# Attention on one core: a written order table in place of a planner, 15 groups on VectorE instead of 16, the last pair dealt differently

## The chip, the cores and the metric

The kernel runs on one core of a Trainium2 chip. The metric is device time in microseconds, from launch to end, as a median of several runs. An execution recorded by the profiler gives the span of the core's instructions as well, and a trace of every instruction.

## The reference

```python
batch, heads, seq, dim = 8, 8, 512, 64            # q, k, v: float32
scale = 1.0 / np.sqrt(q.shape[-1])
scores = np.einsum('bhqd,bhkd->bhqk', q, k) * scale
attn = np.exp(scores - scores.max(axis=-1, keepdims=True))
attn = attn / attn.sum(axis=-1, keepdims=True)
return np.einsum('bhqk,bhkd->bhqd', attn, v).astype(np.float32)
```

There are 64 heads. For each, a 512x512 matrix of scores is formed, its exponential is taken, and the result, divided by its row sums, is multiplied with v.

## The kernel before

**Tiling.** The 64 heads are worked on as 32 pairs (0 to 31), the heads of a pair being a and b. The keys of a head are cut into four chunks of 128. A *block* is the transposed scores of one chunk of one head: 128 keys by 512 queries. Two blocks make a *group* of 128x1024, which is one score buffer (`st`, three of them, two PSUM banks each). In the plain pairs a group holds one chunk of both heads (a0b0, a1b1, a2b2, a3b3); in pair 0 and pair 31 it holds two chunks of one head (a0a1, a2a3, b0b1, b2b3). The two heads' q and k lie in different halves of the 64+64 partitions. There are 128 groups, m = 0 to 127; the last one, b2b3 of pair 31, is done in two halves of 256 queries each, which are steps 127 and 128. Groups 0 to 2 belong to a start written out by hand (`first_pair`).

**Stages, by engine.**
- SyncE loads q, k and v of a pair in 256 KB transfers (`load`, L509) into seven float32 buffers for each of the three, and stores the results from a ring of rows (`store`, L690 for two heads, L694 for one). The last two stores but one go through ScalarE's queue.
- GpSimd casts them to float16 (`cast`, L515 for v, L525 for q and k). `cast_behind` makes a cast wait for a chosen VectorE instruction, so that the two don't work on SBUF at the same time.
- TensorE transposes q and k of a pair (two steps of four, L558), VectorE copies them out of PSUM (`copy`, L565 for pair 1, L571), TensorE forms the scores of a group (two products, L598).
- ScalarE takes the exponential of a group out of PSUM (one instruction, L602, float16 out). For the groups in `ON_DVE` VectorE does this instead: a *raise* that makes float16 bits out of the scores (`raise_`, L625) and five *passes* that mend it (`pass_`, L642, L651, L659, L661, L665). Such a group is left as two factors, `pe` and `pd`, and each of its blocks is multiplied with v twice.
- TensorE multiplies the blocks with v and a column of ones (`values`, L704): a *unit* is one head's 128 queries, four products, and one more for each block that VectorE did. Seven units share a PSUM bank; VectorE takes the reciprocal of their sums (L671) and multiplies (L676). The last head has a path of its own (`last_values`, L720; `finish`, L733 and L734).

**What sets the order.** Every engine works off its own instructions in the order in which the program issues them. Before, the class `Plan` makes that order when the kernel is built: it steps through time with a cost for each operation, and at each step lets each engine choose by its own rules. Its list of steps is worked off in one loop, `for what, *args in steps: do[what](*args)`. A buffer of a pool goes to the next tile when the last reader issued for it has finished. Twelve exponentials (`KNOWN`) are made to wait also for the sixth-last cast issued before them (`OVER`).

The lines that say which groups go to VectorE, and which blocks a group holds:

```python
ON_DVE = (5, 10, 16, 25, 28, 39, 44, 54, 63, 66, 74, 81, 91, 96, 103, 116)
...
        if g in (0, LAST):
            stream += [(g, c, h) for h in range(2) for c in range(NI)]
        else:
            stream += [(g, c, h) for c in range(NI) for h in range(2)]
```

Of the kernel before, what the change touches and what calls it, by code (L numbers as in the profile page):

```python
# [17 lines left out]
class Plan:  # L18

    SLOT, EXP, EXP_DONE, EXP_FIXED = 216, 853, 181, 64  # L20
    INTO, OUT_OF = 96, 96
    TRANSPOSE, V_UNIT = 222, 128
    TO_ACT, TO_DVE, TO_PE = 220, 210, 60

    COPY, NORM, RAISE = (601, 690), (50, 133), (1132, 1215)
    RECIPROCAL = 115
    SCALE, PRODUCT, EXTRA = 333, 600, 29
    COPY_1 = (400, 190)
    NORM_COLUMN, PASS_DONE = 67, 115
    PASSES = (SCALE, SCALE, PRODUCT, SCALE, PRODUCT)  # L30
    BITS = 2
    NEEDS = (None, None, 0, 2, 3)
    FIRST_EXP = 5000
    STEP = 5
    CALM, KEEN = 9000, 4
    FIRST_UNIT = 4
    KNOWN, OVER = (13, 15, 18, 20, 22, 24, 27, 42, 50, 61, 69, 97), 6
    ON_DVE = (5, 10, 16, 25, 28, 39, 44, 54, 63, 66, 74, 81, 91, 96, 103, 116)

    LATE_NORM, LATE_COPY, HURRY, SOON, BACKLOG = 700, 1500, 800, 160, 600  # L40
    LATE_MUL, WAIT = 400, 200
    SLACK, AHEAD = 0, 2

    CAST, CAST_PORT, CAST_DONE, TO_POOL = 557, 475, 130, 150
    SCALE_PORT, PRODUCT_PORT, GAP, REACH = 271, 537, 20, 5
    FIRST_LAND, LOAD, STORE, LATENCY, ISSUE = 5200, 752, 376, 2300, 470
    QUEUED, URGENT = 3500, 16
    PAIRED, STORE_ISSUE = 18, 520
    RAW, QK16, NV, NU = 7, 5, 12, 112
    PAIR, DUEK, DUEV, DUEL, PRE = 3300, 3550, 6000, 5000, 0  # L50

    def __init__(self, groups, pairs, first):
        self.groups, self.pairs = groups, pairs
        self.pe, self.act, self.dve = 7000, self.FIRST_EXP, 6300
        self.pool, self.port, self.dma = 4600, 4600, self.FIRST_LAND
        self.m, self.tiled = first, True
        self.read = []
        self.exps = {}
        for m in range(first):
            self.act += self.EXP + self.EXP_FIXED  # L60
            self.exps[m] = self.act + self.EXP_DONE
            self.read.append(self.exps[m])
        self.tq = {0: 5800}
        self.transposed = {0: 5800}
        self.next_t = 1
        self.part_t = 0
        self.banks = [5100, 5800]
        self.todo = [(g, h) for g in range(pairs) for h in range(2)]
        self.last = self.todo.pop()
        self.last_part = 0  # L70
        self.head = None
        self.units = self.FIRST_UNIT
        self.member = {b: m for m, grp in enumerate(groups) for b in grp}
        self.ready = []
        self.passes = []
        self.passed = {}
        self.raised = set()
        self.steps = []
        self.busy_dve = 0
        self.order, self.paired = [], 0  # L80

        late = {grp[0][0] for m, grp in enumerate(groups) if m in self.ON_DVE}
        due = []
        for g in range(pairs):
            scores = 5000 + self.PAIR * g
            if g:
                due += [(scores - self.DUEK, g, "k"), (scores - self.DUEK + 10, g, "q")]
            due.append((scores + self.DUEV + (self.DUEL if g in late else 0), g, "v"))
        self.due = sorted(due)
        self.uncast = list(self.due)  # L90
        self.casts = []
        self.landed, self.cast_done = {}, {}
        self.first_loads = [(g, n) for _, g, n in self.due if g < self.RAW]
        self.first_loads += [(self.RAW, "k"), (self.RAW, "q")]
        for x in self.first_loads:
            self.dma += self.LOAD
            self.landed[x] = self.dma
        self.loads, self.stores, self.stored = [], [], []
        self.sp = 1650 + 470 * len(self.first_loads)

    def note(self, t, *what):
        self.steps.append((t, len(self.steps)) + what)

    def trigger(self, t):

        ops = self.ops
        if not ops or ops[-1][1] <= t - 300:  # L110
            return 1, None
        n = len(ops) - 1
        while (
            n > 0
            and len(ops) - n < self.REACH
            and not ops[n][2]
            and ops[n][0] - ops[n - 1][1] <= self.GAP
        ):
            n -= 1
        if n > 0 and ops[n][0] - ops[n - 1][1] <= self.GAP:  # L120
            n -= 1
        return len(ops) - n, ops[n][1]

    def emit(self, t, back, after):
        _, g, n = self.uncast.pop(0)
        shared = (g, n) == (1, "q")
        self.note(t, "cast", g, n, back if t > self.CALM else 0)
        if not shared:
            self.casts.append((g, n, t if after is None else after + self.TO_POOL))
        if g + self.RAW < self.pairs:  # L130
            self.loads.append((g + self.RAW, n))

    def fits(self, t, soon=0):
        if not self.uncast:
            return False
        _, g, n = self.uncast[0]
        if n != "v" and g >= self.QK16 and self.transposed.get(g - self.QK16, 1e9) > t:
            return False
        return self.landed.get((g, n), 1e9) <= t + soon

    def step_pool(self, t):
        if self.uncast and self.uncast[0][1:] != (1, "q") and not self.casts and self.pool <= t:
            quiet = not self.passes and self.port <= t and not any(x[1] == "raise" for x in self.ready)
            if self.fits(t) and (quiet or self.uncast[0][0] - self.PRE < t):
                self.emit(t, 1, None)
        if self.casts and self.pool <= t and self.port <= t:
            g, n, after = self.casts[0]
            if after <= t and self.landed.get((g, n), 1e9) <= t:
                self.casts.pop(0)
                begin = max(self.pool, self.port, after, self.landed[(g, n)])  # L150
                self.pool = begin + self.CAST
                self.port = begin + self.CAST_PORT
                self.cast_done[(g, n)] = begin + self.CAST + self.CAST_DONE

    def step_sp(self, t):
        if self.sp > t or (self.loads and self.dma > t + self.QUEUED):
            return
        urgent = len(self.stores) > self.URGENT
        if self.loads and not urgent:
            g, n = self.loads[0]  # L160
            if self.cast_done.get((g - self.RAW, n), 1e9) <= t:
                self.loads.pop(0)
                self.note(t, "load", g, n)
                self.dma = max(self.dma, t + self.LATENCY - self.LOAD) + self.LOAD
                self.landed[(g, n)] = self.dma
                self.sp = t + self.ISSUE
                return
        if self.stores and self.stores[0] <= t:
            both = self.both()
            if both and (len(self.stores) < 2 or self.stores[1] > t):  # L170
                return
            heads = 2 if both else 1
            self.note(t, "store", heads)
            self.dma = max(self.dma, t + self.LATENCY - heads * self.STORE) + heads * self.STORE
            for _ in range(heads):
                self.stores.pop(0)
                self.stored.append(self.dma)
            self.paired += heads - 1
            self.sp = t + self.STORE_ISSUE

    def both(self):

        n = len(self.stored)
        g, h, u = self.order[n]
        return (
            self.paired < self.PAIRED
            and g < self.pairs - 2
            and h == 0
            and n + 1 < len(self.order)
            and self.order[n + 1][0] == g  # L190
            and u % self.NU + 8 <= self.NU
        )

    def room(self, t, u):
        heads = (u - self.NU - self.FIRST_UNIT + 3) // 4
        return heads <= 0 or len(self.stored) >= heads and self.stored[heads - 1] <= t

    def free(self, n=0):
        m = self.m + n
        if m >= len(self.groups):  # L200
            return 1e9
        g = self.groups[m][0][0]
        return max(0 if m < 3 else self.read[m - 3], self.tq.get(g, 1e9))

    def for_dve(self, m):
        return m in self.ON_DVE
# [692 lines left out]
```

## Time and profile before

| | |
|---|---|
| median of 3 runs | 113.71 us (113.62 to 113.92) |
| the profiled execution | 113.92 us |
| its span, first to last instruction | 112.1 us |
| busy: TensorE products, VectorE, ScalarE, GpSimd | 103.2, 100.8, 105.5, 65.9 us |
| granted TensorE clock, mean | 0.994 |
| moved between HBM and SBUF | 25.17 MB read, 8.39 MB written |

The profile shows one execution. Times in it count from the first instruction. PE is TensorE's products, PEld its weight loads, DVE is VectorE, ACT ScalarE, POOL GpSimd, SP SyncE; a q behind an engine's name is its queue of instructions such as DMA issues. A row of a timeline gives the start, the length, the engine, the line of the kernel, the operation, its tiles (out<-in) and how often it came in sequence; square brackets tell how long the engine was idle before it and what ended that. A row of a table of groups gives count, busy time, the mean length of one in ns, and behind the second bar the idle time of the engine before these instructions, with what ended it. A row of busy time by stage gives the stretch and its length, busy time (and count) of PE, PEld, DVE, ACT and POOL, then the granted clock, the DMA engines' share and GB/s.

### The profile page before, as it was taken

What the parts mean: (1) busy time and instruction counts of PE and PEld (TensorE: products, weight loads), DVE (VectorE), ACT (ScalarE), POOL (GpSimd) and SP (SyncE); (2) the same over time, 40 slices, a digit from 0 to 9 for tenths busy, and PEclk for the clock granted to TensorE, in tenths of its full rate; (3) what the DMA queues carried; (4) which work ended last, traced back from release to release, by engine and by line L of the source; (5) the groups of instructions that cost most, each with busy time, mean ns of one, the idle gap of its engine ahead of it and who ended that gap; (6) DMA issues with size and microseconds to landing.
All of it is one profiled execution on the core that took longest, in us unless ns stands there. A gap on an engine that the chain in (4) does not pass through costs nothing.

```text
span 112.1 us, 4408 instructions
## 1 busy us (share of the span) xinstructions
PE 103.2 (92%) x1728; PEld 69.4 (62%) x1728; DVE 100.8 (90%) x227; ACT 105.5 (94%) x118; POOL 65.9 (59%) x127
## 2 busy tenths in 40 slices
PE   7978889999799998999989999899999999999980
PEld 7634555766367766658647767577557577675660
DVE  1647999999999999999999999999999999997390
ACT  4599999999999999999999999999999999999970
POOL 2147768549756886495594786876784855600000
PEclk9999999999999999999999999999999999999997
DMA  3999999999999999999999999999999974142354
GB/s 106 276 359 353 345 350 347 355 336 349 345 347 336 341 346 343 354 364 375 370 358 382 350 355 377 354 372 362 343 366 305 349 245 143 52 141 99 97 167 161
DMA packets 35093, 33.84 MB, mean 302 GB/s; under 512 B 2304, under 2 KB 35072, under 8 KB 35072
## 3 DMA queue, kind: packets, MB, share of 16 engines
q1 hardware_dynamic: 34496, 33.04, 90.4%
q10 hardware_dynamic: 576, 0.52, 1.4%
q8 instruction: 13, 0.21, 0.8%
q14 instruction: 8, 0.07, 0.2%
HBM read 25.17 MB, written 8.39 MB: 299 GB/s over the span
## 4 chain that ended last, share of the span: by engine, by line
DVE 39%; PE 24%; DMA 15%; issue 8%; POOL 7%; SPq 3%; ACT 2%; POOLq 0%; ACTq 0%
PE o L704 13%; DMA v<-in_v_dram 10%; PE st L598 8%; DVE pd L625 8%; DVE tqk L571 7%; DVE ring L676 7%; DMA q<-in_q_dram 5%; DVE m L659 4%; POOL qkp L525 4%; DVE pd L665 4%; POOL vp L515 3%; PE tp L558 2%; SPq L509 2%; DVE m L642 2%; DVE pe L651 2%
## 5 line engine op out<-in xcount | busy, mean ns | idle before, releaser
L602 ACT ACTIVATE pt<-st 128x1024 f16<-128x1024 f32 (+1 forms) x110 | 100.3, 1144 | 0.2 <-PE st L598 0.2
L704 PEld LDWEIGHTS <-pt 128*128 128x128 f16 x880 | 38.8, 98 | 12.1 <-issue 10.2
L704 PE MATMUL o<-vp,pt 128*128 128x65 f16 x880 | 45.3, 194 | 0.4 <-POOL vp L515 0.2
L598 PE MATMUL st<-tqk 64*128 64x512 f16 (+1 forms) x250 | 41.7, 380 | 2.6 <-ACT pt L602 1.4
L525 POOL CAST qkp<-k 128x512 f16<-128x512 f32 x31 | 22.2, 717 | 11.3 <-DVE rc L671 5.3
L525 POOL CAST qkp<-q 128x512 f16<-128x512 f32 x30 | 21.7, 725 | 9.0 <-DVE rc L671 5.3
L515 POOL CAST vp<-v 128x512 f16<-128x512 f32 x32 | 21.4, 679 | 9.2 <-PE st L598 2.4
L676 DVE TENSOR_TENSOR ring<-o,rc 128x448 f32<-128x448 f32 (+2 forms) x37 | 22.3, 606 | 0.4
L704 PE MATMUL o<-vp,pe 128*128 128x65 f16 x128 | 21.8, 194 | 0.0
L704 PE MATMUL o<-vp,pd 128*128 128x65 f16 x128 | 21.7, 192 | 0.0
L558 PE MATMUL tp<-ident,qkp 128*128 128x128 f16 x248 | 19.6, 220 | 1.6 <-DVE tqk L571 0.8
L558 PEld LDWEIGHTS <-qkp 128*128 128x128 f16 x248 | 14.4, 97 | 9.9 <-issue 4.6
L571 DVE COPY tqk<-tp 128x1024 f16<-128x1024 f16 x30 | 20.3, 683 | 0.0
L625 DVE TENSOR_SCALAR pd<-st 128x1024 uint16<-128x1024 f32 x16 | 19.5, 1216 | 0.7 <-PE st L598 0.7
L598 PEld LDWEIGHTS <-tqk 64*128 64x128 f16 x250 | 10.7, 93 | 11.8 <-issue 4.6
L704 PEld LDWEIGHTS <-pe 128*128 128x128 f16 x128 | 12.5, 98 | 3.4 <-issue 3.3
L704 PEld LDWEIGHTS <-pd 128*128 128x128 f16 x128 | 12.5, 98 | 0.0
L659 DVE TENSOR_TENSOR m<-m 128x1024 f16<-128x1024 f16 x16 | 11.0, 685 | 0.0
L665 DVE TENSOR_TENSOR pd<-pd,m 128x1024 f16<-128x1024 f16 x16 | 10.9, 684 | 0.0
L671 DVE RECIPROCAL rc<-o 128x7 f32<-128x7 f32 (+2 forms) x37 | 7.4, 199 | 2.6 <-PE o L704 2.4
L661 DVE TENSOR_SCALAR m<-m 128x1024 f16<-128x1024 f16 x16 | 6.7, 418 | 0.1
L651 DVE TENSOR_SCALAR pe<-pd 128x1024 uint16<-128x1024 uint16 x16 | 6.6, 411 | 0.0
(51 smaller groups left out, 34.9 us busy)
## 6 DMA issues: line engine op xcount, KB each, us to landing
v<-in_v_dram SPq DMA_DIRECT2D x32, 256.0 KB, 5.8
k<-in_k_dram SPq DMA_DIRECT2D x31, 256.0 KB, 5.8
q<-in_q_dram SPq DMA_DIRECT2D x31, 256.0 KB, 5.9
out_dram<-ring SPq DMA_DIRECT2D x18, 256.0 KB, 5.5
out_dram<-ring SPq DMA_DIRECT2D x25, 128.0 KB, 2.2
k<-in_k_dram ACTq DMA_DIRECT2D x2, 128.0 KB, 2.8
q<-in_q_dram SPq DMA_DIRECT2D x2, 128.0 KB, 2.6
out_dram<-ring ACTq DMA_DIRECT2D x2, 128.0 KB, 1.9
```

What stands on the lines that cost most here:

```text
L515: return nc.gpsimd.tensor_copy(out=vps[g % NV][:, :, :, 0:D], in_=raw[g]["v"][:, :, :, :])
L525: return nc.gpsimd.tensor_copy(out=dst, in_=src[:, :, :, :])
L558: reads[g] = nc.tensor.transpose(tps[g][:, n, i, :], qkp[g][:, n, i, :], ident)
L571: nc.vector.tensor_copy(out=tqk[g][:, :, :], in_=tps.pop(g).rearrange("p n i c -> p n (i c)"))
L598: nc.tensor.matmul(st[:, x, cols], kc, qc[:, cols], start=True, stop=True)
L602: ins = nc.scalar.activation(out=pt[:, :, cols], in_=st[:, :, cols], func=EXP, scale=scale, bias=SHIFT)
L625: nc.vector.tensor_scalar(out=r["pd"][:, :, :], in0=r["st"][:, :, :], scalar1=BITS, scalar2=BIAS, op0=AluOp.mult, op1=AluOp.add,)
L651: ins = nc.vector.tensor_scalar(out=r["pe"][:, :, :], in0=u[:, :, :], scalar1=0x7C00, scalar2=None, op0=AluOp.bitwise_and,)
L659: ins = nc.vector.tensor_tensor(out=m16, in0=m16, in1=m16, op=AluOp.mult)
L665: ins = nc.vector.tensor_tensor(out=u16, in0=u16, in1=m16, op=AluOp.mult)
L676: nc.vector.tensor_tensor(out=ring[:, u % NU : u % NU + n, :], in0=o[:, x : x + n, 0:D], in1=rcs.pop(u)[:, 0:n].broadcast_to([P, n, D]), o ...
L704: nc.tensor.matmul(os[u // 7][:, u % 7, :], part[:, y * P : (y + 1) * P], vps[g % NV][:, h, c, :], start=(n == 0), stop=(n == len(parts) - 1),
```

## The change

`Plan` is taken out and a class `Order` put in its place. It holds the order of all engines as text: a letter for each step (`S` scores of the next group, with its exponential if it is ScalarE's; `T` half of the transposes of a pair, `C` its copy; `V` a unit, `L` a part of the last head; `N` reciprocal, `M` multiplication; `R` raise, `a` to `o` passes of three groups in turn; `K` cast, `G` load, `w` and `W` a store of one or two heads; `F` the finish), and lists that say which head, cast, load and PSUM bank is next. With it come these edits:

- `ON_DVE` has 15 groups instead of 16, and most of them at other places; the last is 113 (before: 116).
- The last pair's groups are a0b0, a1b1, a2a3, b2b3 (before: a0a1, a2a3, b0b1, b2b3). Pair 1's are as before.
- The order of heads, casts, loads and stores differs; loads and casts of q, k and v no longer go pair by pair. The loads ahead of the table are the same as before.
- The tiles `pe` and `pd` are taken when the raise is issued, not when the scores are; the VectorE part of the cast of pair 1's q is counted among the instructions that a cast can be put behind. Slices `own:2` stand in the raise and the passes for groups shared between the engines, but there are none (`SPLIT` is empty), so `own` is 0 for a group on VectorE and 2 for one on ScalarE.

```diff
-class Plan:
...
+class Order:
+
+    ON_DVE = (5, 11, 16, 26, 29, 39, 45, 55, 65, 75, 80, 91, 96, 103, 113)
+    SPLIT = ()
+    PAIR_1 = "a0b0 a1b1 a2b2 a3b3"
+    LAST_PAIR = "a0b0 a1b1 a2a3 b2b3"
+    RAW, QK16, NV, NU, FIRST_UNIT, PAIRS = 7, 5, 12, 112, 4, 32
+    WIDE = ()
+    LETTERS = ("abcde", "fghij", "klmno")
+    STEPS = (
+        "SKKTTKCSKSSKRTTKSCVVVaSNcVVSKMSVdTbTKSCKRSKTTKSCVSeTVTfSCKSGRKVSGKVVNGSMKVkSGhVTVGTgViSK"
+        "GCVVSmGSVVNVjVGVVVKMSGSNnVKVMGVVSlGToVTVKVCSKGSNRVKVVVSKMSKGSRKTGTVGKSCGVKVGNaSSKGMTGTcS"
+        "KTCTSfVdVVKCVVVVbGSNSeWVVGVhVVGVMVKSGSNgVKMVVSiVKRTSKTVVCGVKSSGNKTMGSKGTVjVWSKCVGVVKSGRV"
...
+        "fSweSwVVNhVwVVVMVwSNSwiVMVKwVVRSKwTTKSCVKSjVVVVNkSSMKVVVwmVVVwVKNVMSSVwVTTwVVCSSNVMVVVVn"
+        "VwVlVVwSoSVNVVMVVSNwVMVVVVwVVSwNSMVVVVwVVVwSNVMVVVLLwwNLLMFw"
+    )
...
+    CASTS = (
+        "1k 1q 2k 2q 0v 3k2 3q2 4k2 4q3 5k3 5q2 1v2 6k2 3v3 6q2 2v2 7q3 7k3 5v2 4v4 10k4 8k2 8q4 "
+        "9q5 9k2 10q3 11q2 10v2 6v2 12k2 11k5 8v2 13q4 12q2 14q4 7v2 14k4 16q2 13k2 9v2 15q2 16k2 "
...
+    LOADS = (
+        "10k 8k 8q 9k 9q 12k 11q 10q 12q 11k 10v 12v 15k 11v 7v 14q 13q 8v 14k 13v 9v 16q 13k 20q "
+        "17q 18q 15q 16k 17v 19k 14v 17k 18k 20k 15v 23k 22k 21v 22q 19q 21q 21k 18v 24k 23q 16v "
...
+    def steps(self):
...
+        for step in self.STEPS:
+            if step == "S":
+                yield "scores", m, m in self.ON_DVE
+                m += 1
...
+    special = {0: "a0a1a2a3b0b1b2b3", 1: Order.PAIR_1, LAST: Order.LAST_PAIR}
+    plain = "".join(f"a{c}b{c}" for c in range(NI))
     stream = []
     for g in range(NP):
-        if g in (0, LAST):
-            stream += [(g, c, h) for h in range(2) for c in range(NI)]
-        else:
-            stream += [(g, c, h) for c in range(NI) for h in range(2)]
+        for h, c in re.findall(r"([ab])(\d)", special.get(g, plain)):
+            stream.append((g, int(c), "ab".index(h)))
...
-        plan = Plan(groups, NP, 3)
-        steps = plan.run()
+        order = Order()
         first_loads()
-        for g, name in plan.first_loads:
+        for g, name, _ in order.read(order.FIRST):
             load(g, name)
...
-        for what, *args in steps:
+        for what, *args in order.steps():
             do[what](*args)
```

More of the change, by code (lines that the diff above doesn't have):

```diff
@@ L1 @@
 import math
+import re
 from contextlib import ExitStack
@@ new lines, with read @@
+class Order:
[7 more added lines that the diff above has]
+    STEPS = (
+        "SKKTTKCSKSSRKTTKSCVVVaSNcVVSKMSVdTbTKSCKRSKTTKSCVSeTVTfSCKSGRKVSGKVVNGSMKVkSGhVTVGTgViSK"
+        "GCVVSmGSVVNVjVGVVVKMSGSNnVKVMGVVSlGToVTVKVCSKGSNRVKVVVSKMSKGSRKTGTVGKSCGVKVGNaSSKGMTGTcS"
+        "KTCTSfVdVVKCVVVVbGSNSeWVVGVhVVGVMVKSGSNgVKMVVSiVKRTSKTVVCGVKSSGNKTMGSKGTVjVWSKCVGVVKSGRV"
+        "VGKVSWNVkVGVMSGVmSGTlTGnVVCSKSNGaKMSToVVVVcVTVVCKSSNdVGVMVKVSbVGKRSVKVGTSGNSMTGSCKWVGeSG"
+        "TgTVGfVKVCVVVKGSNSMKWVVVhVGVTTWiVSKCGVSjVSKNVMVKSRVVKVVSKGTNTMKWSSCGKTTGkVKVCGVSGmVVGVVn"
+        "SGNTlGTKMSWSCKVVVoVVVVKSNSMKVVRVKSVKVVVKSNSMTKTaTKTCSSCGVVGVRVKSGVVWVSbGVNVcVVGSGVdVVMGK"
+        "SSNfTKMGTSeVGVVKCVVGVKVSGNgTKMTSWhVVVGCSKSVGiVKVVVWVNKSMwKSRTKWVSTwjVSkSwCVKVWVSNKMVVGVR"
+        "SKTVKTSCKVVVmSSNlTTKMSnGVVbVwVaVVKCVWSKSNWVMVKGSRVKGVTSwVoTWSCVVwSNgGTKMSGTcWSVCVVWVVdVV"
+        "fSweSwVVNhVwVVVMVwSNSwiVMVKwVVRSKwTTKSCVKSjVVVVNkSSMKVVVwmVVVwVKNVMSSVwVTTwVVCSSNVMVVVVn"
+        "VwVlVVwSoSVNVVMVVSNwVMVVVVwVVSwNSMVVVVwVVVwSNVMVVVLLwwNLLMFw"
+    )
+    HEADS = (
[3 rows of a table added]
+    )
+    CASTS = (
[6 rows of a table added]
+    )
+    FIRST = "1k 1q 2k 2q 0v 3k 3q 4k 4q 5k 5q 1v 3v 6k 6q 2v 5v 4v 6v 7k 7q"
+    LOADS = (
[4 rows of a table added]
+    )
+    BANKS_T = "0100011001110011010010110110000"
+    BANKS_V = "0101010100110010110100010011010101010"
+    @staticmethod
+    def read(text):
+        found = re.findall(r"(\d+)([a-z])(\d*)", text)
+        return [(int(g), n, int(x or 0)) for g, n, x in found]
+    def steps(self):
+        m, g, part, u, last = 3, 1, 0, self.FIRST_UNIT, 0
+        end = self.FIRST_UNIT + 8 * self.PAIRS - 4
+        copied, loads, casts = 1, iter(self.read(self.LOADS)), iter(self.read(self.CASTS))
+        heads = [(x, "ab".index(h)) for x, h, _ in self.read(self.HEADS)]
+        begins = [self.FIRST_UNIT] + list(range(7, end, 7))
+        bundles = [(a, b - a, int(x)) for a, b, x in zip(begins, begins[1:] + [end], self.BANKS_V)]
+        recs, muls = iter(bundles), iter(bundles)
+        raises = iter(self.ON_DVE)
+        units = [x for x in self.ON_DVE if x not in dict(self.WIDE)]
+        todo = {}
+        for step in self.STEPS:
+            if step == "S":
+                yield "scores", m, m in self.ON_DVE
+                m += 1
+            elif step == "T":
+                yield "transposes", g, part, int(self.BANKS_T[g - 1])
+                g, part = g + part, 1 - part
+            elif step == "V":
+                h = heads[(u - self.FIRST_UNIT) // 4]
+                yield "values", *h, (u - self.FIRST_UNIT) % 4, u, bundles[u // 7][2]
+                u += 1
+            elif step == "L":
+                yield "last", last
+                last += 1
+            elif step == "C":
+                yield "copy", copied, 0
+                copied += 1
+            elif step == "N":
+                yield "rec", *next(recs)
+            elif step == "M":
+                yield "mul", *next(muls)
+            elif step == "R":
+                yield "raise", next(raises)
+            elif step == "F":
+                yield ("finish",)
+            elif step == "K":
+                yield "cast", *next(casts)
+            elif step == "G":
+                yield "load", *next(loads)[:2]
+            elif step in "wW":
+                yield "store", 1 + (step == "W")
+            else:
+                n = [step in x for x in self.LETTERS].index(True)
+                s = self.LETTERS[n].index(step)
+                seen = todo.setdefault((n, s), iter(units[n::3]))
+                yield "pass", next(seen), s
@@ L463 @@
     dpool = ctx.enter_context(tc.tile_pool(name="pd", bufs=4))
-    wpool = ctx.enter_context(tc.tile_pool(name="work", bufs=Plan.BITS))
+    wpool = ctx.enter_context(tc.tile_pool(name="work", bufs=2))
     opool = ctx.enter_context(tc.tile_pool(name="out", bufs=4))
@@ L580, in scores @@
         st = ps_st.tile([P, 2, S], FP32, tag="st", name=f"st_{m}")
+        own = 0 if on_dve and m not in Order.SPLIT else 1 if on_dve else 2
         if on_dve:
-            tiles = {n: dpool.tile([P, 2, S], U16, tag=n, name=f"{n}_{m}") for n in ("pe", "pd")}
-            raised[m] = {"st": st, **tiles}
-            parts = [tiles[n].bitcast(FP16) for n in ("pe", "pd")]
+            raised[m] = {"st": st, "own": own}
+        if own == 0:
+            pass
         elif half == 1:
@@ L598, in scores @@
             nc.tensor.matmul(st[:, x, cols], kc, qc[:, cols], start=True, stop=True)
-            blocks[(g, c, h)] = [part[:, x, :] for part in parts] if on_dve else [pt[:, x, :]]
-        if on_dve:
+            if x < own:
+                blocks[(g, c, h)] = [pt[:, x, :]]
+        if own == 0:
             return
         ins = nc.scalar.activation(
-            out=pt[:, :, cols], in_=st[:, :, cols], func=EXP, scale=scale, bias=SHIFT
+            out=pt[:, 0:own, cols], in_=st[:, 0:own, cols], func=EXP, scale=scale, bias=SHIFT
         )
-        if m in Plan.KNOWN:
-            tc.add_manual_dep(ins.ins, behind_it[-Plan.OVER].ins.name, SYNC, reason="cast")
+        if m in KNOWN:
+            tc.add_manual_dep(ins.ins, behind_it[-OVER].ins.name, SYNC, reason="cast")
     FIRST, LINEAR, CUBIC = 0.4580331, 1.0167876, 0.1665620
@@ L623, in raise_ @@
         r = raised[m]
+        for n in ("pe", "pd"):
+            r[n] = dpool.tile([P, 2, S], U16, tag=n, name=f"{n}_{m}")
+        own = r["own"]
+        for x, b in enumerate(groups[m]):
+            if x >= own:
+                blocks[b] = [r[n].bitcast(FP16)[:, x, :] for n in ("pe", "pd")]
         dve(
             nc.vector.tensor_scalar(
-                out=r["pd"][:, :, :],
-                in0=r["st"][:, :, :],
+                out=r["pd"][:, own:2, :],
+                in0=r["st"][:, own:2, :],
                 scalar1=BITS,
@@ L638, in pass_ @@
             r["m"] = wpool.tile([P, 2, S], U16, tag="m", name=f"m_{m}")
-        u, m16 = r["pd"], r["m"].bitcast(FP16)[:, :, :]
-        u16 = u.bitcast(FP16)[:, :, :]
+        own = r["own"]
+        u = r["pd"]
+        u16 = u.bitcast(FP16)[:, own:2, :]
+        if s != 1:
+            m16 = r["m"].bitcast(FP16)[:, own:2, :]
         if s == 0:
             ins = nc.vector.tensor_scalar(
-                out=r["m"][:, :, :],
-                in0=u[:, :, :],
+                out=r["m"][:, own:2, :],
+                in0=u[:, own:2, :],
                 scalar1=0x03FF,
@@ L651, in pass_ @@
             ins = nc.vector.tensor_scalar(
-                out=r["pe"][:, :, :],
-                in0=u[:, :, :],
+                out=r["pe"][:, own:2, :],
+                in0=u[:, own:2, :],
                 scalar1=0x7C00,
@@ L691, in store @@
             return
-        left = 2 * NP - 1 - (u0 + NI - Plan.FIRST_UNIT) // NI
+        left = 2 * NP - 1 - (u0 + NI - Order.FIRST_UNIT) // NI
         queue = nc.scalar if left < 2 else nc.sync
```

390 lines of the change are left out of this document (9 added, 381 removed), and 9 rows, old and new, of tables (CASTS, HEADS, LOADS).

## The prediction

> **What bounds the kernel now.** I read the page first, then the busy time by stage, then ScalarE's timeline, then the end of the chain of waits.
>
> ```profile
> span 112.1 us, 4408 instructions
> PE 103.2 (92%) x1728; PEld 69.4 (62%) x1728; DVE 100.8 (90%) x227; ACT 105.5 (94%) x118; POOL 65.9 (59%) x127
> DVE 39%; PE 24%; DMA 15%; issue 8%; POOL 7%; SPq 3%; ACT 2%; POOLq 0%; ACTq 0%
> L602 ACT ACTIVATE pt<-st 128x1024 f16<-128x1024 f32 (+1 forms) x110 | 100.3, 1144 | 0.2 <-PE st L598 0.2
> 10.00:30.00 20.00, 18.34 (x277) 11.53 (x274) 19.86 (x40) 20.00 (x23) 14.21 (x27) 1.00 1.09 347
> 30.00:60.00 30.00, 29.04 (x495) 19.62 (x492) 29.93 (x62) 30.00 (x34) 21.09 (x42) 1.00 1.09 354
> 60.00:88.00 28.00, 27.43 (x484) 18.54 (x480) 27.86 (x58) 28.00 (x31) 20.36 (x38) 1.00 1.07 355
> 88.00:108.00 20.00, 19.49 (x374) 13.47 (x372) 17.43 (x41) 20.00 (x24) 6.47 (x12) 1.00 0.44 145
> ```
>
> Three engines are over 90%, and the chain names VectorE (39%) and TensorE (24%) rather than ScalarE (2%). The chain misleads here: it goes back through whoever released the last wait, and where several engines run in step it may stay with any of them. The stages decide (each row: stretch, length, then PE, PEld, DVE, ACT, POOL busy): ScalarE is busy 20.00 of 20, 30.00 of 30, 28.00 of 28 and 20.00 of 20 us, and no other engine is. Its exponentials of line 602 waited 0.2 us in the whole run. ScalarE is a closed queue from first exponential to last:
>
> ```profile
> 5.20 0.60 ACT L801 ACTIVATE pt<-st_0a 128x512 f16<-128x512 f32 x1 [0.43 <-PE st_0a L794]
> 5.69 0.59 ACT L801 ACTIVATE pt<-st_0b 128x512 f16<-128x512 f32 x1
> 6.17 1.95 ACT L801 ACTIVATE pt<-st 128x1024 f16<-128x1024 f32 x2
> 7.98 1.06 ACT L602 ACTIVATE pt<-st 128x1024 f16<-128x1024 f32 x1
> 9.21 2.90 ACT L602 ACTIVATE pt<-st 128x1024 f16<-128x1024 f32 x3 [0.18 <-PE st L598]
> ...
> 9.21 99.28 ACT L602 ACTIVATE pt<-st 128x1024 f16<-128x1024 f32 x109 [0.18 <-PE st L598]
> ```
>
> (The fifth row is the start of the sixth.) The last exponential ends at 9.21 + 99.28 = 108.49, and what follows hangs on it alone:
>
> ```profile
> 108.55 0.31 PE o_last L720 x4
> 108.86 0.02 issue
> 108.89 0.19 DVE rc_last L733
> 109.08 0.02 issue
> 109.10 0.42 DVE obl L734
> ...
> 109.55 0.33 SPq L740 DMA_DIRECT2D out_dram<-obl  x1
> ```
>
> Four products start 0.06 us after it, then one reciprocal, one multiplication, one store; the span ends at 112.1, 3.6 us after ScalarE. So time = ScalarE's start + its exponentials + its waits + 3.6 us, and each part of the change is asked what it does to these four.
>
> **The change part by part.**
>
> *One group fewer on VectorE.* There are 126 score steps after the first pair, the last two of half size. Before, 16 go to VectorE and 110 to ScalarE (x110 above); the new `ON_DVE` has 15 numbers, so ScalarE gets 111, and the new one is a full 128x1024. Price: the 109 in the row of 99.28 us are 107 full and 2 halves. A half costs 0.49 (5.69 less 5.20), so a full one costs (99.28 - 0.98)/107 = 0.92. The pair from 6.17 gives the same: it ends at 8.12, the half before at 6.28, and 1.84/2 = 0.92. Each lasts over 1 us in its own row but overlaps the next; the distance between ends counts. **+0.92 us, on the path**, as ScalarE has no idle time to put it in.
>
> The Trainium skill, "ScalarE: Activation LUTs", section "What ACT_TABLE_LOAD costs", gives 186 ns + 0.833 ns an element with about 93 ns of overlap back to back, and 93 ns more for a pointer operand: estimates of 0.95 and 1.04 us at 1024 elements, by which the sum would be +0.95 or +1.04. The measured 0.92 is below both, and it is what I use.
>
> *What VectorE and TensorE are spared.*
>
> ```profile
> L625 DVE TENSOR_SCALAR pd<-st 128x1024 uint16<-128x1024 f32 x16 | 19.5, 1216 | 0.7 <-PE st L598 0.7
> L642 DVE TENSOR_SCALAR m<-pd 128x1024 uint16<-128x1024 uint16 x16 | 6.5, 408 | 0.0
> L651 DVE TENSOR_SCALAR pe<-pd 128x1024 uint16<-128x1024 uint16 x16 | 6.6, 411 | 0.0
> L659 DVE TENSOR_TENSOR m<-m 128x1024 f16<-128x1024 f16 x16 | 11.0, 685 | 0.0
> L661 DVE TENSOR_SCALAR m<-m 128x1024 f16<-128x1024 f16 x16 | 6.7, 418 | 0.1
> L665 DVE TENSOR_TENSOR pd<-pd,m 128x1024 f16<-128x1024 f16 x16 | 10.9, 684 | 0.0
> 33.23 0.54 PE st L598 x4
> 33.77 1.40 PE o L704 x40
> 36.45 0.55 PE tp L558 x8
> ```
>
> A group on VectorE costs it 1.22 + 0.41 + 0.41 + 0.69 + 0.42 + 0.68 = 3.8 us. Its two blocks are each multiplied twice (`pe` and `pd`): 2 x 4 further products at 1.40/40 = 0.035 us, so 0.28 us of TensorE goes too. Both lie under the closed ScalarE queue: worth 0. Were that cover gone, they would be worth up to 3.8 us; that is the faster rival.
>
> *The last pair dealt anew.* Before, all its groups hold two blocks of one head; now two of the four hold one block of each, as everywhere else. The rows have no clean pair of same-head products; four of mixed heads take 0.54. I bound the gain by 0 and 0.54 us of TensorE for the two groups together, and take 0, as the scores wait for ScalarE to free their buffer. The end is the same in both orders: four `V` and four `L` behind the last `S`, then `F`; the last `L` needs the second half of b2b3. So the 3.6 us stay, and the two stores on ScalarE's queue still stand behind its last exponential.
>
> *The start.* From the end of group 3 (7.98 + 1.06 = 9.04) to that of the third exponential after it (12.11) are 3.07 us for 3 x 0.92 = 2.76: 0.31 us lost, ScalarE's only real wait. TensorE there:
>
> ```profile
> 8.78 0.82 PE L598 MATMUL st<-tqk 64*128 64x512 f16 x6 [0.52 <-DVE tqk L565]
> 9.54 0.62 PE L558 MATMUL tp<-ident,qkp 128*128 128x128 f16 x8
> 10.31 0.42 PE L704 MATMUL o<-vp,pt 128*128 128x65 f16 x8 [0.16 <-POOL vp L515]
> 10.66 0.39 PE L598 MATMUL st<-tqk 64*128 64x512 f16 x2
> ```
>
> Group 4 waits for pair 1's copies. A row starts 0.11 before the one ahead of it ends (0.60 less 0.49), so 9.21 stands for 9.04 - 0.11 = 8.93: 0.28 of the 0.31. The new table has the same steps there (S, two T, C, S, S, S) and the same first loads, so that stays. Group 7's scores came behind two value units that waited for the first v; the new table puts them right behind the transposes. **-0.03 us.** Ends: 0 and -0.31.
>
> *The table of TensorE.* Up to three groups of scores stand ready for ScalarE (three buffers), 2.76 us of its work. The longest stretches that I count between two scores in the new table (ahead of groups 53 and 61) are 28 value products and 8 transposes: 28 x 0.035 + 0.55 = 1.53 us, and the scores behind them 0.54 at most. That fits under 2.76, and also under 1.84, which is left where one of the three is VectorE's, if the scores are a mixed pair (half of 0.54). Cost 0; bounds 0 and some 0.3 us where such a stretch meets a late buffer, the size of the early loss above.
>
> *VectorE's order, and its tiles taken in the raise.* The raise of each group holds a score buffer behind whatever VectorE has queued. Scores that waited:
>
> ```profile
> L598 PE MATMUL st<-tqk 64*128 64x512 f16 (+1 forms) x250 | 41.7, 380 | 2.6 <-ACT pt L602 1.4 <-DVE pd L625 0.7 <-DVE tqk L565 0.5
> ```
>
> 0.7 us of waiting for 16 raises, none of it seen by ScalarE after the start. Fifteen raises: 0, between 0 and one raise over one exponential, 1.22 - 0.92 = 0.30 us, for each that comes badly.
>
> *Loads, casts and stores in another order.* This is what is least sure.
>
> ```profile
> L525 POOL CAST qkp<-q 128x512 f16<-128x512 f32 x30 | 21.7, 725 | 9.0 <-DVE rc L671 5.3 <-DVE m L642 0.9 <-DMA q<-in_q_dram 0.8
> q<-in_q_dram SPq DMA_DIRECT2D x31, 256.0 KB, 5.9
> DMA to landing us min/median/max: 2.3/5.8/6.6
> ```
>
> A load needs a free one of seven buffers. In the new table the tightest is q of pair 15: the cast that frees its buffer (13q) stands behind group 41, its own behind group 51, ten groups. A group takes (108.49 - 9.21)/125 = 0.79 us, so 7.9 us, against a landing of at most 6.6 and a cast of 0.73: 0.6 us over. All other loads have 15 groups (11.9 us) or more. A late 15q holds GpSimd and the casts behind it, but pair 15 is transposed only after group 56, another 4.0 us. Cost 0; bounds 0 and, with a landing of 5.8 on top, 5.8 - 4.6 = 1.2 us. Twelve exponentials also wait for the sixth-last cast; the nearest of these stands six groups (4.7 us) ahead, so 0.
>
> *The sum.* +0.92 - 0.03 = +0.89. On the profiled execution: 113.92 + 0.89 = 114.81, its span 113.0. That run is 0.21 above the median of the runs, 113.71, so **114.6** as a median. The runs of before lie within 0.3 us; I call 0.3% (0.34 us) what can be told from no change.
>
> **The rivals.**
>
> 1. *A late load empties the stock (slower yet).* Mechanism and price as above: +0.89 + 1.2, 115.8. For it: the DMA engines moved 347 to 355 GB/s up to 88 us and the new table has less lead in places. Against: GpSimd's q casts lost only 0.8 us to loads.
> 2. *A raise or a long stretch of TensorE comes late once or twice.* +0.89 + 0.3 to 0.6: 114.9 to 115.2. For it: a written order that no engine can leave. Against: less work on both engines.
> 3. *Faster: VectorE is the true bound.* VectorE is busy 29.93 of 30 us and leads the chain. If ScalarE only keeps up with it, one group less takes 3.8 off VectorE and gives 0.92 to ScalarE: at best -2.9, 110.8. The point at which it decides is a wait of ScalarE of over 0.92 us that the change can remove; the rows show 0.31, most of it before VectorE's first group. The Trainium skill, same page, "Rules for kernel authors", has `exp` belong to ScalarE alone, which speaks for moving a group back. [...]
> 4. *No difference.* All of the 0.31 at the start vanishes: +0.92 - 0.31 = +0.61, 114.3, still over 0.34. It takes a first exponential 0.3 us earlier as well, but the first loads and the first pair are the same. Nor can the change fail to do what it says: the table has 15 `R`, 75 passes and 126 `S`.
>
> **How the numbers follow.** ScalarE alone, 114.3 to 114.9: 0.70. Rival 2: 0.12. Rival 1 or worse: 0.10. No difference: 0.04. Faster: 0.04. The first three are all slower: 0.92. The forecast is 114.6; the range goes from just below rival 4's time, 114.2, up to rival 1's 115.8.
>
> **What would show it.** Right: line 602 x111 with its idle time near 0.2, last exponential ending near 109.4, the same row of four products 0.06 us behind it, 3.6 us from there to the end; VectorE under 100 us, the rows of lines 625 to 665 at x15, and group 7's exponential without a gap. Wrong towards slower: line 602 with idle time of a microsecond, released by the scores, and behind that GpSimd waiting for `in_q_dram` near 45 us, or the scores for `pd`. Wrong towards faster: a full exponential that takes less than 0.92 from end to end, or a tail shorter than 3.6 us.

## The result and the profile after

The changed kernel takes 114.45 us (median; 114.19 to 115.18), the kernel before 113.86 in the same series (113.52 to 114.36). The ratio is 1.0065, 95% interval 1.0036 to 1.0093: slower by 0.6 to 0.7 us. Forecast were 114.6 and +0.89.

The page of the changed kernel, then its four stages (columns as before), then ScalarE's timeline:

```profile
span 113.3 us, 4335 instructions
PE 105.6 (93%) x1720; PEld 70.7 (62%) x1720; DVE 100.6 (89%) x221; ACT 106.2 (94%) x119; POOL 62.9 (56%) x127
PE 71%; ACT 9%; DVE 9%; DMA 3%; issue 2%; POOL 1%; SPq 0%; ACTq 0%
L292 ACT ACTIVATE pt<-st 128x1024 f16<-128x1024 f32 (+1 forms) x111 | 101.0, 1254 | 0.0
```

```profile
10.00:30.00 20.00, 18.97 (x275) 11.61 (x273) 19.79 (x40) 20.00 (x24) 14.43 (x28) 1.00 1.09 347
30.00:60.00 30.00, 29.33 (x490) 19.91 (x489) 29.63 (x60) 30.00 (x34) 20.10 (x41) 1.00 1.08 355
60.00:88.00 28.00, 27.80 (x464) 18.52 (x460) 27.08 (x55) 28.00 (x32) 19.41 (x41) 1.00 1.07 354
88.00:108.00 20.00, 20.00 (x375) 14.00 (x372) 17.51 (x39) 20.00 (x24) 4.92 (x9) 1.00 0.44 143
```

```profile
5.35 0.60 ACT L500 ACTIVATE pt<-st_0a 128x512 f16<-128x512 f32 x1 [0.51 <-PE st_0a L493]
8.13 101.04 ACT L292 ACTIVATE pt<-st 128x1024 f16<-128x1024 f32 x111
```

Line 292 is line 602 of before. It has one exponential more (x111) and now no idle time at all, the row of 101.04 us is in one piece, and the stages again show ScalarE full throughout; in the last one TensorE is full too (20.00 of 20 us, before 19.49). The chain has moved from VectorE (39%) to TensorE (71%), though the bound is the same; its shares say little here. The last exponential ends at 8.13 + 101.04 = 109.17, before at 108.49.

This first profile is of an execution of 115.12 us, 0.67 above the median; a second one, of 114.29 us, is shown in experiment 2. The first is longer because it began 0.24 later (5.35 against 5.11) and because the last store landed later: from the last exponential to the end of the span it has 113.3 - 109.2 = 4.1 us, the second 112.5 - 108.9 = 3.6, as before.

### The profile page after: what moved, and what is told of

Its sections match the earlier page's. It is cut to its first block, busy times and chain, and to the rows that moved or that the text cites. A ratio compares the mean times of both kernels' runs of the same rounds, so it can differ in the third digit from the quotient of the medians.

```text
span 113.3 us, 4335 instructions
## 1 busy us (share of the span) xinstructions
PE 105.6 (93%) x1720; PEld 70.7 (62%) x1720; DVE 100.6 (89%) x221; ACT 106.2 (94%) x119; POOL 62.9 (56%) x127
## 4 chain that ended last, share of the span: by engine, by line
PE 71%; ACT 9%; DVE 9%; DMA 3%; issue 2%; POOL 1%; SPq 0%; ACTq 0%
PE o L403 31%; PE st L287 27%; PE tp L246 11%; ACT pt L292 9%; DVE pd L321 3%; DMA q<-in_q_dram 3%; DVE tqk L259 2%; POOL qkp L213 1%; DVE ring L375 1%; PE st L493 1%; DVE tqk L253 1%; DVE m L358 1%; DVE m L360 0%; DVE obl L433 0%; ACT q L468 0%
## 5 line engine op out<-in xcount | busy, mean ns | idle before, releaser
L403 PE MATMUL o<-vp,pt 128*128 128x65 f16 x888 | 48.0, 195 | 0.3 <-POOL mark L231 0.2
L287 PE MATMUL st<-tqk 64*128 64x512 f16 (+1 forms) x250 | 44.5, 381 | 2.4 <-ACT pt L292 0.6
L213 POOL CAST qkp<-k 128x512 f16<-128x512 f32 x31 | 20.8, 675 | 10.5 <-DVE m L358 3.7
L213 POOL CAST qkp<-q 128x512 f16<-128x512 f32 x30 | 19.5, 660 | 6.5 <-DVE m L360 2.0
L287 PEld LDWEIGHTS <-tqk 64*128 64x128 f16 x250 | 12.6, 93 | 13.3 <-issue 3.7
L246 PE MATMUL tp<-ident,qkp 128*128 128x128 f16 x248 | 20.8, 220 | 0.0
L403 PE MATMUL o<-vp,pe 128*128 128x65 f16 x120 | 20.8, 195 | 0.0
L403 PE MATMUL o<-vp,pd 128*128 128x65 f16 x120 | 20.6, 192 | 0.0
L321 DVE TENSOR_SCALAR pd<-st 128x1024 uint16<-128x1024 f32 x15 | 18.2, 1211 | 0.7 <-PE st L287 0.7
L341 DVE TENSOR_SCALAR m<-pd 128x1024 uint16<-128x1024 uint16 x15 | 6.3, 418 | 0.0
```

The lines of the kernel that those rows point to most:

```text
L213: return nc.gpsimd.tensor_copy(out=dst, in_=src[:, :, :, :])
L246: reads[g] = nc.tensor.transpose(tps[g][:, n, i, :], qkp[g][:, n, i, :], ident)
L287: nc.tensor.matmul(st[:, x, cols], kc, qc[:, cols], start=True, stop=True)
L321: nc.vector.tensor_scalar(out=r["pd"][:, own:2, :], in0=r["st"][:, own:2, :], scalar1=BITS, scalar2=BIAS, op0=AluOp.mult, op1=AluOp.add,)
L403: nc.tensor.matmul(os[u // 7][:, u % 7, :], part[:, y * P : (y + 1) * P], vps[g % NV][:, h, c, :], start=(n == 0), stop=(n == len(parts) - 1),
```

## The experiments

The theory: ScalarE is a closed queue, and the time is its start, the number of its exponentials times 0.917 us, its waits, and 3.6 us. The rivals: VectorE is the true bound; or the written order costs or earns by itself. Each experiment was timed in rounds beside the kernel before, whose median was 113.80 us for experiments 1 to 4, 113.91 for 5 to 8 and 113.69 for 9 to 11. Differences are to that median of the same series; the changed kernel stood at +0.59 and +0.68 in its two series. It was not timed again beside experiments 5 to 11, so what is said there against it carries the difference between series, some 0.1 us.

**1 and 2. Both kernels again, for second profiles.** No edit.

> The kernel before, unchanged, for a second profile and for what two series of one kernel differ by. ScalarE theory: the ratio is 1.000 within 0.3%, line 602 x110 at 0.917 us from end to end. Open is its loss at the start: 0.31 us in the first profile. If that belongs to the order, it comes back, 0.25 to 0.35 us with the sixth and seventh exponentials late again; if it hangs on when the first q and k land, it differs, 0 to 0.3 us.

> The changed kernel, unchanged, for a second profile. ScalarE theory: +0.6 to +0.9 us (ratio 1.005 to 1.008), no idle time in line 292 after the first two. Open is its tail: 4.1 us from the last exponential to the end of the span, where before has 3.6. If that belongs to the order of the last stores it comes back at 4.0 to 4.2; if it hangs on the landing of one store it is 3.5 to 4.1.

Measured: before 113.79 us, ratio 0.998 (0.996 to 1.001). Changed kernel 114.48 us, ratio 1.0044 (1.0016 to 1.0071). ScalarE's timeline and VectorE's cast of pair 1's q, of before and then of the changed kernel:

```profile
5.01 0.60 ACT L801 ACTIVATE pt<-st_0a 128x512 f16<-128x512 f32 x1 [0.29 <-PE st_0a L794]
7.27 0.29 DVE L523 CAST qkp<-q 128x256 f16<-128x256 f32 x1 [1.24 <-DMA q<-in_q_dram]
9.12 99.47 ACT L602 ACTIVATE pt<-st 128x1024 f16<-128x1024 f32 x109 [0.28 <-PE st L598]
```

```profile
5.11 0.60 ACT L500 ACTIVATE pt<-st_0a 128x512 f16<-128x512 f32 x1 [0.51 <-PE st_0a L493]
6.93 0.29 DVE L211 CAST qkp<-q 128x256 f16<-128x256 f32 x1 [0.53 <-DMA q<-in_q_dram]
7.89 101.03 ACT L292 ACTIVATE pt<-st 128x1024 f16<-128x1024 f32 x111
```

From first exponential to last: before 108.49 - 5.20 = 103.29 and 108.59 - 5.01 = 103.58; changed 103.82 and 108.92 - 5.11 = 103.81. The changed kernel's 101.03 and 101.04 us are 109 full exponentials of 0.917, two halves of 0.49 and the 0.1 by which the first starts before the one ahead of it ends: no wait in either profile. Its stretch is longer by only 0.23 to 0.53 rather than 0.92, so before contains 0.4 to 0.7 us of waits that the changed kernel hasn't. Measured from end to end of neighbouring exponentials they are 0.34 us in the first profile of before and 0.70 in the second: 0.29 and 0.38 at group 4, 0.05 and 0.02 at group 7, and in the second a further 0.29 between groups 24 and 46, in pieces of 0.03 to 0.13.

The wait at group 4 hangs on when q of pair 1 lands, and not on the order. Up to 10 us both kernels issue the same instructions in the same order on every engine, and in all thirteen profiles of this study the load of that q is issued at 2.11 or 2.12 us; it lands between 6.61 and 7.50. What counts is how long after ScalarE's first exponential VectorE's cast of it begins. Where that is at least 2.14 us, group 4 waits, and the wait is that delay less 1.88 us, within 0.01, in either order: 7.37 - 5.20 = 2.17 and 0.29, 7.27 - 5.01 = 2.26 and 0.38 in the profiles of before, 2.39 and 0.51 in experiment 7, which has the table. Where it is at most 1.82 us, as in both profiles of the changed kernel (6.83 - 5.35 = 1.48 and 6.93 - 5.11 = 1.82), there is no wait. The wait (0.25 to 0.51 us) is there in four of the six profiles that start in the planner's order, and in two of the seven with the table. Why one execution's q lands later than another's stays open.

(In the kernel the first line of `STEPS` begins `SKKTTKCSKSSRKTT`: the first raise `R` stands ahead of the cast `K` beside it, and not behind it as in the diff shown above.)

**3. Before, with 15 groups.**

```diff
-    ON_DVE = (5, 10, 16, 25, 28, 39, 44, 54, 63, 66, 74, 81, 91, 96, 103, 116)
+    ON_DVE = (5, 10, 16, 25, 28, 39, 44, 54, 63, 66, 74, 81, 91, 96, 103)
```

> The kernel before with group 116 struck from the list of VectorE, nothing else; its planner makes the order anew for 15 groups. ScalarE theory: one more full exponential, +0.92 us against before (0 to -0.1 for the rest), ratio 1.007 to 1.008. Theory of VectorE as the bound: 3.8 us less work there, faster by up to 2.9 us. Theory that the order is what costs: no difference.

Measured: 114.58 us, +0.78, ratio 1.0067 (1.0037 to 1.0097). One group handed back to ScalarE, with nothing else of the change (the planner makes its order anew for 15 groups), costs what the whole change costs. VectorE as the bound is out for the removal. The table costs nothing that can be told from noise beside the planner's order with as many groups: 114.48 in the same series against 114.58.

**4. Changed kernel, with 14 groups.**

```diff
-    ON_DVE = (... 96, 103, 113)
+    ON_DVE = (... 96, 103)          # and its R and five passes struck from STEPS
```

> The changed kernel with group 113 taken from VectorE too, 14 groups: one R and five passes struck from the table, all else in its place. ScalarE theory: another +0.92 us against the changed kernel, +1.5 to +1.8 against before. Theory of VectorE as the bound: faster than the changed kernel by up to 2.9 us.

Measured: 115.37 us, +1.57, ratio 1.0119 (1.0079 to 1.0160): 0.89 us above the changed kernel. ScalarE's row, again in one piece:

```profile
7.75 101.95 ACT L292 ACTIVATE pt<-st 128x1024 f16<-128x1024 f32 x112
```

101.95 less 101.03 is 0.92, one exponential.

**5 and 6. The last pair's deal by itself.** In 5 the changed kernel gets the old deal (the edit shown), in 6 the kernel before gets the new one, by the same change of its list of blocks the other way.

```diff
-    LAST_PAIR = "a0b0 a1b1 a2a3 b2b3"
+    LAST_PAIR = "a0a1 a2a3 b0b1 b2b3"
```

> The changed kernel with the last pair dealt as before (a0a1, a2a3, b0b1, b2b3), the table as it is. ScalarE theory: the same time as the changed kernel within 0.2 us, +0.5 to +0.9 against before; TensorE loses up to 0.5 us that ScalarE covers. Rival, the new deal earned something at the end: 0.3 to 0.6 us slower than the changed kernel.

> The kernel before with the last pair dealt as in the changed one and nothing else; 16 groups, the planner makes the order anew. ScalarE theory: as many exponentials as before, so the same time within 0.2 us. Rival, the deal is worth 0.3 us or more at the end: 113.5 or less.

Measured: 5 takes 115.09 us, +1.18, ratio 1.0101 (1.0059 to 1.0142), so some 0.5 above the changed kernel; 6 takes 113.94, ratio 1.001 (0.998 to 1.004). In the planner's order the deal earns nothing that can be told from noise. In the table the old deal costs: the ScalarE theory's 0 was wrong, the rival's 0.3 to 0.6 came. First ScalarE and two scores steps of 5, then the same steps in the second profile of the changed kernel:

```profile
8.04 101.33 ACT L292 ACTIVATE pt<-st 128x1024 f16<-128x1024 f32 x111
104.89 0.60 PE L287 MATMUL st<-tqk 64*128 64x512 f16 x2
108.35 0.39 PE L287 MATMUL st<-tqk 64*128 64x256 f16 x2
```

```profile
104.54 0.39 PE L287 MATMUL st<-tqk 64*128 64x512 f16 x2
107.59 0.39 PE L287 MATMUL st<-tqk 64*128 64x256 f16 x2
```

Two products of one head take 0.60 us, two of both heads 0.39. The scores of the last half come at 108.35 rather than 107.59, and ScalarE's row is 0.30 longer, 0.10 before and 0.20 at the last halves. The tail is longer too, 3.77 us for 3.59, since TensorE comes to its last products later. The Trainium skill, "TensorEngine Tiling (Array Packing)", section "Theoretical Speedup", gives up to 2x for a dimension of 64 or less; these products, which contract over 64, show 0.60 against 0.39, 1.5x.

In the kernel before, two of the last pair's same-head groups, a2a3 and b0b1, come one right behind the other, and their four products run side by side:

```profile
104.87 0.61 PE L598 MATMUL st<-tqk 64*128 64x512 f16 x4
```

Four take 0.61 us there, where the table, with value units between the two groups, pays 0.60 for each two. With a0a1 (0.60) the three groups cost TensorE 1.21 us in the old deal; in 6, with the new one, they cost 0.39 + 0.82 = 1.21. So the planner's order had nothing to gain there.

**7 and 11. More work for VectorE.** The second pass of nine groups is issued twice, in the changed kernel (7) and in the one before (11).

```diff
         dve(ins)
+        if s == 1 and m in Order.ON_DVE[3:12]:      # 11: Plan.ON_DVE[3:12]
+            nc.vector.tensor_scalar(out=r["pe"]..., in0=u..., scalar1=0x7C00, op0=AluOp.bitwise_and)
```

> The changed kernel with the second pass (float16 exponent bits, 0.41 us) of nine VectorE groups done twice, 3.7 us more work for VectorE, which is what the dropped group spared it. ScalarE theory: 0 to +0.3 us against the changed kernel, since the spared work was under cover. Theory of VectorE as the bound: +3 us or more.

> The kernel before with the second pass of nine VectorE groups done twice, 3.7 us more for VectorE, the same dose that cost the changed kernel 5.2 us. If the dropped group left the changed kernel a reserve on VectorE, before pays more, +6 to +9 us. If the new order gave the reserve away, before pays the same, +4.5 to +6.

Measured: 7 takes 119.71 us, +5.80, some 5.1 above the changed kernel; 11 takes 119.95, +6.26. Of 7, the added group, the stages (columns as before), and what ScalarE and TensorE waited for (us in total, times, longest):

```profile
L367 DVE TENSOR_SCALAR pe<-pd 128x1024 uint16<-128x1024 uint16 x9 | 5.3, 588 | 0.3
```

```profile
30.00:60.00 30.00, 27.18 (x444) 17.66 (x440) 29.61 (x61) 28.23 (x31) 17.46 (x34) 1.00 1.01 321
60.00:88.00 28.00, 25.80 (x426) 16.77 (x423) 27.31 (x52) 26.85 (x29) 19.45 (x40) 1.00 1.03 332
```

```profile
ACT pt L292 <- PE st L287: 3.8, 9, 0.7
PE o L411 <- DVE ring L383: 2.5, 4, 0.9
PE st L287 <- DVE tqk L259: 1.0, 2, 0.6
```

The nine took 0.59 us each, 5.3 together, not the 3.7 I had planned, and the time rose by nearly all of it. VectorE is no fuller than before the dose (29.61 of 30); it is ScalarE that now has holes (28.23 of 30), since TensorE waits for VectorE, above all to empty a bank (`ring`; no such wait in the second profile of the changed kernel, where it waited 0.8 us for `tqk`, the copy of a pair). So under this order VectorE has no reserve in the middle of the kernel. Of 11:

```profile
L668 DVE TENSOR_SCALAR pe<-pd 128x1024 uint16<-128x1024 uint16 x9 | 5.6, 621 | 0.3
```

5.6 us added for 6.3. That lies just inside the range that I gave for a reserve, +6 to +9. But the kernel before pays only about 1 us more than the changed one, for a dose 0.3 larger: the reserve that the dropped group left is below 1 us, not 3.8. The added pass was not entered among the instructions that GpSimd's casts are put behind, and that made the dose larger than planned. It took 0.43 us in seven of the eighteen cases and 0.71 to 0.72 in the other eleven, and in every one of the eleven a GpSimd cast ran at the same time; of the seven, five ran without one, and in the other two the cast took 0.87 us. Of the 5.3 us in 7, 3.8 are thus nine passes of 0.43 and 1.5 the collisions.

**8. One group shared.** Group 115 of the changed kernel: first block to ScalarE, second to VectorE.

```diff
-    ON_DVE = (... 103, 113)
-    SPLIT = ()
+    ON_DVE = (... 103, 113, 115)
+    SPLIT = (115,)                  # R behind the scores of 116, a to e behind groups 123 to 126
```

> The changed kernel with group 115 shared: ScalarE does its first block (512 columns, 0.49 us instead of 0.92), VectorE the second (about 2.2 us more for it, put where it had idle time, near the end). ScalarE theory: -0.43 us against the changed kernel, +0.1 to +0.4 against before. Theory of VectorE as the bound: slower than the changed kernel by up to 2.2 us.

Measured: 115.55 us, +1.64, ratio 1.0142 (1.0101 to 1.0182); 1 us slower than the changed kernel where 0.43 faster was expected. ScalarE's row breaks once:

```profile
7.87 92.54 ACT L292 ACTIVATE pt<-st 128x1024 f16<-128x1024 f32 x101
101.22 8.78 ACT L292 ACTIVATE pt<-st 128x1024 f16<-128x1024 f32 x10 [0.81 <-PE st L287]
```

The half exponential is saved, but a place in the queues is lost. VectorE, GpSimd and TensorE of 8 in that stretch, then GpSimd in the second profile of the changed kernel:

```profile
97.70 0.69 DVE L321 TENSOR_SCALAR pd<-st 128x512 uint16<-128x512 f32 x1 [0.58 <-ACT pt L292]
99.02 0.37 DVE L341 TENSOR_SCALAR m<-pd 128x1024 uint16<-128x1024 uint16 x1
99.45 1.63 POOL L203 CAST vp<-v 128x512 f16<-128x512 f32 x2 [2.26 <-DVE m L341]
100.12 0.67 PE L403 MATMUL o<-vp,pt 128*128 128x65 f16 x16 [0.41 <-POOL vp L203]
100.73 0.61 PE L287 MATMUL st<-tqk 64*128 64x512 f16 x4
```

```profile
98.07 1.63 POOL L203 CAST vp<-v 128x512 f16<-128x512 f32 x2 [1.09 <-DVE m L341]
```

The added raise waits 0.58 us and holds VectorE's queue; a pass behind it comes late, with it the cast of a v that is put behind that pass, with it TensorE's units, and behind them the scores. ScalarE loses 0.92 us there and 0.25 near the end; another 0.25 went at group 4 to a late q. It is one try at one place: it shows what an instruction more in VectorE's queue can cost, not that sharing can't pay.

**9 and 10. Less work for VectorE.** The fourth pass of nine groups is left out, in the changed kernel (9) and in the one before (10).

```diff
+        elif s == 3 and m in Order.ON_DVE[3:12]:     # 10: Plan.ON_DVE[3:12]
+            return
         elif s == 3:
```

> The changed kernel without the fourth pass (the cubic's linear step, 0.42 us) of nine VectorE groups: 3.8 us less for VectorE, as much as the change itself took off; it leaves out part of the exponential there. ScalarE theory: 0 to -0.1 us against the changed kernel, +0.5 to +0.9 against before, since ScalarE has not one wait left in it. Theory of VectorE as the bound (it is without reserve when work is added): faster than the changed kernel by 1 us or more.

> The kernel before without the fourth pass of nine VectorE groups, 3.8 us less for VectorE; it leaves out part of the exponential there. ScalarE theory: at most what ScalarE lost in waits behind its first few exponentials, 0.05 to 0.35 us, so 0 to -0.35 us; line 602 still x110 at 0.917. If those waits come from VectorE being late, they go; if they come from how the planner deals TensorE's work, they stay and the time is the same. Theory of VectorE as the bound: -1 to -3.8 us.

Measured: 9 takes 114.47 us, +0.78, ratio 1.0062 (1.0037 to 1.0087), the changed kernel's time; 10 takes 113.98, ratio 1.0006 (0.998 to 1.003), the time of before. In 9:

```profile
30.00:60.00 30.00, 29.32 (x494) 19.90 (x492) 28.02 (x56) 30.00 (x34) 19.91 (x41) 1.00 1.07 352
60.00:88.00 28.00, 27.82 (x460) 18.43 (x456) 25.78 (x50) 28.00 (x32) 19.30 (x41) 1.00 1.02 335
7.94 101.04 ACT L292 ACTIVATE pt<-st 128x1024 f16<-128x1024 f32 x111
```

VectorE really is freer (28.02 and 25.78 us for 29.63 and 27.08), and ScalarE's row has the same 101.04 us. Taking 3.8 us of passes off VectorE is worth nothing in either kernel; adding 5.3 costs 5.1. In 10 ScalarE waits 0.43 us at group 4, with a late q, and still at groups 31 and 46 (0.09 us), but not around 24; but these waits differ between two executions of before as well, so which part is VectorE's stays open.

## Why the prediction was right

*The bound* was read rightly from the stages, against the chain of waits. Experiments 3 and 4 hand one group from VectorE to ScalarE and cost 0.78 and 0.89 us; 9 and 10 take work from VectorE alone and gain nothing. The cost is that of the added exponential.

*+0.92 for one exponential.* Shown: 101.95 less 101.03 is 0.92. The estimates of 0.95 to 1.04 from the Trainium skill ("ScalarE: Activation LUTs", "What ACT_TABLE_LOAD costs") are too high for back-to-back exponentials here, which stand 0.917 apart from end to end.

*-0.03 at the start: too small, and in the profiles the reason the sum came out high.* Measured were +0.59 and +0.68, 0.2 to 0.3 below +0.89. Group 7's wait went as said. But I took before's other waits from one profile and let them stay. The wait at group 4 is not a fixed term, as I had it: it hangs on when q of pair 1 lands, and was missing in both profiles of the changed kernel. And the planner's order has further waits between groups 17 and 46, 0 to 0.6 us by profile (none in the first, 0.29 in experiment 1, 0.22 in 3, 0.60 in 6, 0.10 in 10), which the one profile I had did not show; the table has none there in the profiles of experiments 2, 4, 5 and 9. In the profiles that is what the new order earns, against 0.92; in the medians, 114.48 against 114.58 with as many groups (experiment 3), it can't be told from noise. What share the late q and these waits each have in the medians isn't settled. As far as it is the q, the gain is luck of the landing and not a merit of the table.

*VectorE and TensorE under cover, worth 0.* Right for what was taken away. But I priced the loss of that cover as if VectorE had room under it, and expected 0 to 0.3 us of the dose in experiment 7; it cost 5.1. In the middle both engines stand near their limit (from 30 to 60 us ScalarE 30.00 of 30, VectorE 29.63): ScalarE sets the floor, and VectorE has little room under it. A whole group more on VectorE there can then be expected to cost, which no run here tries. Experiment 8 failed at another point: from 88 to 108 us VectorE has idle time in the changed kernel (17.51 of 20), but TensorE has none (20.00 of 20), and the added raise made it wait for a cast of v. The detail "VectorE under 100 us" was wrong too: 100.6 after 100.8. The rows of the raise and the passes sum to 3.0 us less, but two of the fifth passes ran beside GpSimd casts and took 960 and 1115 ns, where before none took over 703:

```profile
L364 DVE TENSOR_TENSOR pd<-pd,m x15: 640/684/1115, 15.5 to 103.5; 128x1024 f16<-128x1024 f16 x15
```

(the row of line 364, min/median/max in ns.) The rest of the missing 3.8 lies in rows that overlap less, which I have not followed.

*The last pair dealt anew, worth 0 (bounds 0 and 0.54).* Right for the planner's order (6), wrong for the table (5), where the old deal costs about 0.5 us, 0.30 of it as waits of ScalarE and 0.18 as a longer tail. The bound held it; the value taken did not. The cover that I named, the scores waiting for ScalarE to free their buffer, is gone in the last stage of the table, where TensorE has no idle time. Nor is it so that the rows of before have no clean pair of same-head products: `102.98 0.60 PE st L598 x2`, on its chain, is one.

*The tail* of 3.6 us stayed, in the second profile. In the table two ends meet there: the reciprocal of the last head waits for the multiplication before it (109.11 + 0.42 = 109.53, next at 109.56).

*The rivals.* A late load: no wait of ScalarE behind its first exponential in either profile of the changed kernel, so not seen. But the tightest load was not the one I named. In the first profile GpSimd's longest wait for a q, 1.0 us, was for pair 7's, at 22.14 us; q of pair 15 landed 1.8 us before its cast. A late raise: not seen either, until experiment 8 put one in. Faster by VectorE: refuted by 9 and 10. No difference: a ratio of 1 lies below the lower end of both intervals. But the mechanism of that rival came in both profiles of the changed kernel, where the whole wait at the start is gone, and its +0.61 is nearer to the measured +0.59 and +0.68 than my +0.89. I had tied it to a first exponential 0.3 us earlier; in the profiles that came later (5.35 and 5.11 for 5.20 and 5.01), and the q earlier.

## What to carry to other kernels

Where several engines are over 90% busy, find the one that is full in every stage and count its instructions; a chain of waits may name any of the others. Test the others in both directions: that taking work from an engine is worth nothing doesn't mean that it has room for more. And look at waits in two or three profiles before pricing one as a term of the order, as a transfer's landing can make and unmake it.

## What the runs showed of the hardware that I had not expected

A load issued by the same instruction at the same time landed up to 0.9 us apart between executions (q of pair 1, issued at 2.11 or 2.12 us, landed between 6.61 and 7.50 in thirteen profiles), enough to give or take up to 0.51 us of a closed queue. The last store of the first profile of the changed kernel took 0.5 us longer to land than that of the second (2.20 us from its issue, and 1.69), with the same order ahead of it. And a VectorE pass of 0.43 us took 0.72 in eleven of eighteen cases, each with a GpSimd cast running beside it.
